# A twelve-layer float32 network on one core: the order of Strassen pairs and second-product units in the FFN blocks

## The chip, the core and the metric

The program runs on one core of one Trainium2 chip. The metric is the device time of one execution in microseconds (us), the median of several runs. TensorE (PE in the views) multiplies; its weight loads are listed apart as PEld. VectorE (DVE), ScalarE (ACT) and GpSimd (POOL) work element by element, and SyncE (SP) issues most of the DMAs. Each engine runs its own instructions in the order in which they were written, and waits at the first one whose inputs are not there.

## The reference

`x` is 512 tokens of 1024 features in float32. A first network of four layers (a gated linear recurrence, a spatial gating unit, a short convolution, a second recurrence) is followed by a second network of one layer (an RWKV-7 scan beside dilated attention, then cross attention to a memory). Every one of the five layers ends in the same feed-forward block (FFN):

```
def _sqrelu_mlp(h, w1, w2):
    return jnp.square(jax.nn.relu(h @ w1)) @ w2      # w1: 1024 x 4096, w2: 4096 x 1024

x = x + mix
x = x + _sqrelu_mlp(_rmsnorm(x, norm_mlp_g[i]), mlp_w1[i], mlp_w2[i])
```

The second network's block is the same with its own names (`ffn_w1_2`, `ffn_w2_2`), and the result is normed once more at the end. The change touches these five FFN blocks alone.

## The kernel before

Activations lie feature by token: a tile of 128 features x 512 tokens fills one of 75 equal slots in SBUF (tag "A", NSLOT = 75), or one of 8 PSUM banks. A float32 product is made of three reduced-precision ones: every operand is split into a rounded part and a rest (hi and lo), and `mm3` issues hi*hi (L896), hi*lo (L897) and lo*hi (L898). Weights come from HBM as float32 `raw` tiles, are rounded on ACT into `whi` (L839 for a whole unit of 128x1024, L825 for half a unit) and the rest goes into `wlo` on DVE (L840, L807).

An FFN block, `ffn`, works in four quarters of 1024 hidden features. `us[q]` holds quarter q as eight tiles, each as `uhi`/`ulo`.

- The first quarter's eight first-product units are plain products (`mm`).
- The other 24 come as 12 Strassen **pairs** (`pair`, letter P in the table): two hidden tiles by seven products of half width (84 matmuls of 128x256; operands `thi`, `tlo`). DVE forms four sums of weight tiles (`ws`, L796 and L798) and seven `wlo`; as products end, DVE adds them up (`cm` L1074 and L1075, `tu` L1078, `cy` L1080 and L1083), ACT does relu (L940), square (L1005) and the rounding into `uhi` (L1006), and DVE makes `ulo` (L1009). A pair's tile j+1 is finished from `tu`, tile j last, from `cy`.
- The second product is made of **units** (`unit`, letter U): 24 matmuls of 128x512 over the eight tiles of `us[q]`, then DVE adds the bank to `x` (L1093). Eight units per quarter. `late` makes a unit of quarters 1 to 3 read the tiles in the order 0..5, 7, 6, since 7 and 6 are finished last.

What stands where is written out by hand: three groups, one per quarter q = 0, 1, 2, each with the eight units of quarter q and the four pairs that make quarter q + 1, in the order of a string of twelve letters (line 1110). After the third group `project` runs the eight units of quarter 3. Within group 0, units also drive `side`, which forms the Strassen operands from the normed input.

Weights are readied ahead: `_next` prepares (rounds) units up to two places ahead of the one in use (PREP = 2, a place is a unit or two products of a pair), and issues loads on SP in the order of use, with at most two whole units and two pairs of raw weights in flight. Stages of several threads (the recurrence layers, the second network's mixing stage and its cross attention) are ordered by a planner (`schedule`), which follows a modelled clock through the whole program; an FFN block has one thread, so its order is only the string's.

Of the kernel before, what the change touches and what calls it, by code (L numbers as in the profile page):

```python
# [651 lines left out]
class Net:  # L652
# [340 lines left out]
    def ffn(self, inp, nxt, w1, w2):  # L993
# [64 lines left out]
        def pair(s0, s1, u, j, last):  # L1058

            a, b = HALF  # L1060
            ps, add = {}, nc.vector.tensor_add
            for i, (k, bank, h) in enumerate(PRODUCTS):
                w = self.w_pair(s0, s1, i)
                while todo and todo[0][0] <= i:
                    todo.pop(0)[1]()
                if h == 0:
                    ps[bank] = self.psum()
                for c in range(4):
                    self.mm3(ps[bank][:, HALF[h]], w[0][:, c], w[1][:, c], *op[k, c], c == 0, c == 3, 357)
                if i == 1:  # L1070
                    y, m = self.t("cy"), self.t("cm")
                    nc.scalar.copy(y[:, a], ps[0][:, a])
                elif i == 2:
                    add(m[:, a], y[:, a], ps[0][:, b])  # L1074
                    add(m[:, b], m[:, a], ps[1][:, a])  # L1075
                elif i == 4:
                    t = self.t("tu")
                    add(t.rearrange("p (c n) -> p c n", c=2), m[:, None, b].to_broadcast([P, 2, 256]),  # L1078
                        ps[2].rearrange("p (c n) -> p c n", c=2))
                    add(y[:, b], m[:, a], ps[2][:, b])  # L1080
                    todo.extend(relu2(t, u, j + 1, (5, 6)))
                elif i == 6:
                    add(y, y, ps[3])  # L1083
                    todo.extend(relu2(y, u, j, (0, 1)))
                    if last:
                        while todo:
                            todo.pop(0)[1]()
                self.lock(i < 6)
                yield

        def unit(q, m):
            ps = yield from self.mm(w2[q][m], us[q], ks=late if q else None)
            nc.vector.tensor_add(self.x[m], self.x[m], ps)  # L1093
            yield
# [12 lines left out]
            yield  # L1107
        for q in range(3):
            u, j, m = us[q + 1], 0, 0
            for step in "UUUUUUPUUPPP" if q == 0 else "UUUUPUUPUUPP":  # L1110
                if step == "P":
                    yield from pair(w1[q * 8 + 8 + j], w1[q * 8 + 9 + j], u, j, j == 6)
                    j += 2
                    continue
                for n, need in enumerate(unit(q, m)):
                    if n % 2 == 1 and todo:
                        todo.pop(0)[1]()
                    if q == 0 and n % 2 == 0:
                        next(side, None)
                    yield need  # L1120
                m += 1
            us[q] = None
# [1056 lines left out]
```

## Time and profile before

| | |
|---|---|
| median of 3 runs | 3479.54 us (3474.63 to 3480.76) |
| profiled execution, its own time | 3475.65 us |
| its span in the trace | 3473.8 us |
| TensorE busy | 3377.3 us, 97% of the span |
| VectorE busy | 2308.4 us, 66% |
| ScalarE busy | 1529.3 us, 44% |
| granted TensorE clock, mean | 0.993 of full speed |

The profiled execution took 3475.65 us, of which the span holds 3473.8; it lies inside the range of the timed runs. PE's busy time hardly tells stages apart: matmuls are pipelined, each is recorded longer than it advances the engine, so what a stretch costs is read from the starts of its first matmul and of the one behind it.

### The profile page before, as it was taken

How to read it: one execution, taken by the hardware profiler on the slowest of the kernel's cores; microseconds unless marked ns; L12 is line 12 of the kernel's file. 1: busy time of each engine (PE TensorE's matmuls, PEld its weight loads, DVE VectorE, ACT ScalarE, POOL GpSimd, SP SyncE). 2: the span in 40 equal slices, each digit the busy share in tenths (PEclk: the TensorE clock that was granted, in tenths of full speed). 3: DMA queues.
4: the chain of work that ended last, by engine and by line, in shares of the span. 5: the costliest groups of instructions: out<-in, count | busy, mean ns of one | idle time of the engine just before them, and what ended most of it. 6: DMA issues, size and time to landing. Idle time of an engine off the chain costs nothing. (4 is left out here: it accounts for less than half of the span.)

```text
span 3473.8 us, 48153 instructions
## 1 busy us (share of the span) xinstructions
PE 3377.3 (97%) x18850; PEld 2778.3 (80%) x18850; DVE 2308.4 (66%) x3618; ACT 1529.3 (44%) x2391; POOL 521.4 (15%) x845
## 2 busy tenths in 40 slices
PE   8999999999999999999999999999999999999998
PEld 6778888888887888888877888777767787778887
DVE  7677666567666567666767666776567666567665
ACT  5634444345443234444554445443354344334444
POOL 1020002210001010002010001556245400110002
PEclk9999999999999999999999999999999999999999
DMA  3223332232333333332224232332224245223331
GB/s 119 87 85 115 97 98 83 84 94 92 98 98 104 97 91 103 98 98 91 82 85 133 73 98 85 109 90 85 73 82 127 87 121 173 64 76 122 94 100 62
DMA packets 127236, 334.90 MB, mean 96 GB/s; under 512 B 18592, under 2 KB 21792, under 8 KB 127008
## 3 DMA queue, kind: packets, MB, share of 16 engines
q1 hardware_dynamic: 119712, 322.37, 30.0%
q0 software_dynamic: 7296, 9.46, 1.1%
q8 instruction: 148, 2.42, 0.3%
q14 instruction: 80, 0.66, 0.1%
HBM read 317.07 MB, written 14.68 MB: 95 GB/s over the span
## 5 line engine op out<-in xcount | busy, mean ns | idle before, releaser
L840 DVE TENSOR_TENSOR wlo<-raw,whi 128x1024 fp32r<-128x1024 f32 (+3 forms) x466 | 608.9, 1307 | 279.3 <-ACT whi L839 270.3
L896 PE MATMUL ps<-hhi,whi 128*128 128x512 f32 x1512 | 619.1, 409 | 11.2 <-ACT whi L839 6.9
L898 PE MATMUL ps<-hhi,wlo 128*128 128x512 f32 x1512 | 598.8, 396 | 7.3 <-DVE wlo L840 7.3
L897 PE MATMUL ps<-hlo,whi 128*128 128x512 f32 x1512 | 599.0, 396 | 5.7 <-DVE hlo L476 5.7
L839 ACT CAST whi<-raw 128x1024 fp32r<-128x1024 f32 (+3 forms) x466 | 463.8, 999 | 309.9 <-PE ps L897 181.7
L896 PE MATMUL ps<-uhi,whi 128*128 128x512 f32 (+1 forms) x1296 | 511.5, 395 | 16.1 <-ACT uhi L1006 16.1
L897 PE MATMUL ps<-ulo,whi 128*128 128x512 f32 (+1 forms) x1296 | 511.3, 395 | 6.1 <-DVE ulo L1009 6.1
L898 PE MATMUL ps<-uhi,wlo 128*128 128x512 f32 (+1 forms) x1296 | 509.6, 393 | 0.0
L898 PE MATMUL ps<-thi,wlo 128*128 128x256 f32 x1680 | 475.1, 283 | 7.8 <-DVE wlo L807 7.1
L897 PE MATMUL ps<-tlo,whi 128*128 128x256 f32 x1680 | 471.8, 281 | 0.0
L896 PE MATMUL ps<-thi,whi 128*128 128x256 f32 x1680 | 471.1, 280 | 0.0
L896 PEld LDWEIGHTS ps<-hhi,whi 128*128 128x128 f32 x1512 | 285.2, 189 | 85.0 <-ACT whi L839 6.9
L898 PEld LDWEIGHTS ps<-hhi,wlo 128*128 128x128 f32 x1512 | 285.1, 189 | 76.2 <-DVE wlo L840 9.0
L897 PEld LDWEIGHTS ps<-hlo,whi 128*128 128x128 f32 x1512 | 285.1, 189 | 71.6 <-DVE hlo L476 10.5
L898 PEld LDWEIGHTS ps<-thi,wlo 128*128 128x128 f32 x1680 | 316.3, 188 | 13.9 <-DVE wlo L807 13.9
L896 PEld LDWEIGHTS ps<-thi,whi 128*128 128x128 f32 x1680 | 316.8, 189 | 1.8
L897 PEld LDWEIGHTS ps<-tlo,whi 128*128 128x128 f32 x1680 | 316.1, 188 | 1.8
L896 PEld LDWEIGHTS ps<-uhi,whi 128*128 128x128 f32 x1296 | 244.9, 189 | 76.5 <-ACT uhi L1006 22.6
L897 PEld LDWEIGHTS ps<-ulo,whi 128*128 128x128 f32 x1296 | 244.9, 189 | 67.1 <-DVE ulo L1009 13.1
L825 ACT CAST whi<-ws 128x512 fp32r<-128x512 f32 x240 | 149.0, 621 | 323.0 <-DVE ws L798 169.6
L898 PEld LDWEIGHTS ps<-uhi,wlo 128*128 128x128 f32 x1296 | 244.8, 189 | 55.7
L897 PE MATMUL ps<-lo,whi 128*128 128x512 f32 x616 | 245.5, 398 | 7.1 <-DVE lo L1258 4.5
(363 smaller groups left out, 4984.2 us busy)
## 6 DMA issues: line engine op xcount, KB each, us to landing
raw<-in_mlp_dram SPq DMA_DIRECT2D x160, 512.0 KB, 3.6
raw<-in_mlp_dram SPq DMA_DIRECT2D x192, 256.0 KB, 5.6
raw<-in_u_ffn_w_dram SPq DMA_DIRECT2D x40, 512.0 KB, 3.6
raw<-in_a_win_dram SPq DMA_DIRECT2D x39, 512.0 KB, 3.6
raw<-in_w_rest_dram SPq DMA_DIRECT2D x34, 512.0 KB, 3.7
raw<-in_w_rkv_dram SPq DMA_DIRECT2D x26, 512.0 KB, 3.6
raw<-in_c_win_dram SPq DMA_DIRECT2D x24, 512.0 KB, 3.6
raw<-in_u_ffn_w_dram SPq DMA_DIRECT2D x48, 256.0 KB, 5.6
```

The source lines that it names most:

```text
L825: nc.scalar.copy(h, w)
L839: nc.scalar.copy(h[:, c], r[:, c])
L840: nc.vector.tensor_sub(l[:, c], r[:, c], rt(h[:, c]))
L896: nc.tensor.matmul(ps, wh, xh, start=start, stop=False)
L897: nc.tensor.matmul(ps, wh, xl, start=False, stop=False)
L898: nc.tensor.matmul(ps, wl, xh, start=False, stop=stop)
```

## The change

The letters are put in another order. In group 0, `UUUUUUPUUPPP` becomes `UUUUUPUPUPPU`; in groups 1 and 2, `UUUUPUUPUUPP` becomes `UUUUPUPUPUPU`. The numbers of units (8) and pairs (4) in a group stay, and each group now ends with a unit.

```
-            for step in "UUUUUUPUUPPP" if q == 0 else "UUUUPUUPUUPP":
+            for step in "UUUUUPUPUPPU" if q == 0 else "UUUUPUPUPUPU":
```

In the built program the places look like this.

ACT in the first FFN block, from the last pair of group 0 to the first unit of group 1, before (`whi<-raw 128x1024` is the rounding of a unit's weights, `tu` and `cy` end in the two hidden tiles):

```order
L1072 COPY cy<-ps 128x256
L825 CAST whi<-ws 128x512
L839 CAST whi<-raw 128x1024
L940 ACTIVATE tu<-tu 128x512
L1005 ACTIVATE tu<-tu 128x512
L1006 CAST uhi<-tu 128x512
L839 CAST whi<-raw 128x1024
L940 ACTIVATE cy<-cy 128x512
L1005 ACTIVATE cy<-cy 128x512
L1006 CAST uhi<-cy 128x512
```

The same place now:

```order
L1072 COPY cy<-ps 128x256
L839 CAST whi<-raw 128x1024 x2
L940 ACTIVATE tu<-tu 128x512
L1005 ACTIVATE tu<-tu 128x512
L1006 CAST uhi<-tu 128x512
L940 ACTIVATE cy<-cy 128x512
L1005 ACTIVATE cy<-cy 128x512
L1006 CAST uhi<-cy 128x512
L839 CAST whi<-raw 128x1024 x3
```

The unit of group 0 that now stands behind the pair, and the first one of group 1, have both been rounded before the pair's last tiles come, and no rounding of a unit stands between the two tiles any more.

DVE in group 1 of the same block, from the `tu` of the first pair on, before, where two units follow (`x<-x,ps` closes a unit):

```order
L1078 TENSOR_TENSOR tu<-cm,ps 128x512
L1080 TENSOR_TENSOR cy<-cm,ps 128x256
L840 TENSOR_TENSOR wlo<-raw,whi 128x1024
L1009 TENSOR_TENSOR ulo<-tu,uhi 128x512
L1083 TENSOR_TENSOR cy<-cy,ps 128x512
L796 TENSOR_TENSOR ws<-raw 128x512
L798 TENSOR_TENSOR ws<-ws,raw 128x512
L807 TENSOR_TENSOR wlo<-raw,whi 128x512
L798 TENSOR_TENSOR ws<-raw 128x512
L1009 TENSOR_TENSOR ulo<-cy,uhi 128x512
L1093 TENSOR_TENSOR x<-x,ps 128x512
```

The same place now, where one unit follows and then the next pair:

```order
L1078 TENSOR_TENSOR tu<-cm,ps 128x512
L1080 TENSOR_TENSOR cy<-cm,ps 128x256
L796 TENSOR_TENSOR ws<-raw 128x512
L798 TENSOR_TENSOR ws<-ws,raw 128x512
L807 TENSOR_TENSOR wlo<-raw,whi 128x512
L798 TENSOR_TENSOR ws<-raw 128x512
L1009 TENSOR_TENSOR ulo<-tu,uhi 128x512
L1083 TENSOR_TENSOR cy<-cy,ps 128x512
L807 TENSOR_TENSOR wlo<-ws,whi 128x512 x2
L1009 TENSOR_TENSOR ulo<-cy,uhi 128x512
L1093 TENSOR_TENSOR x<-x,ps 128x512
```

The next pair's first weight sums have moved ahead of this pair's last additions.

The planner's clock reaches the second network's mixing stage at another moment, and there it chooses another order; one place on ACT (`p` is a projected tile, + is now, - is before):

```order
-L1481 ACTIVATE p<-z,vec 128x512
 L1481 ACTIVATE p<-z,vec 32x512
 L839 CAST whi<-raw 128x1024
+L1481 ACTIVATE p<-z,vec 128x512
+L939 ACT_TABLE_LOAD
+L940 ACTIVATE p<-p 128x512
+L940 ACTIVATE p<-p 32x512
+L945 CAST hi<-p 128x512
+L945 CAST hi<-p 32x512
 L1634 COPY bkT<-ps 128x512
```

An activation has moved ahead of the copies, and brings a load of ACT's function table with it; there are two more such loads in the whole program. The recurrence layers keep their order.

## Rows read from the trace of the kernel before

**Rows 1.** The page's part 1: engine, busy us, share, instructions.
```profile
PE 3377.3 (97%) x18850; PEld 2778.3 (80%) x18850; DVE 2308.4 (66%) x3618; ACT 1529.3 (44%) x2391; POOL 521.4 (15%) x845
```
**Rows 2.** Who waited for whom, PE alone, whole run: total, times, longest.
```profile
PE ps L896 <- ACT uhi L1006: 16.1, 15, 1.8
...
PE ps L898 <- DVE wlo L807: 7.1, 25, 0.5
PE ps L897 <- DVE ulo L1009: 6.1, 19, 0.6
```
**Rows 3.** Stretches: length, busy PE, PEld, DVE, ACT, POOL, clock, DMA, GB/s; 2190.07: mixing.
```profile
282.98:591.51 308.53, 302.41 (x1778) 264.49 (x1776) 208.99 (x314) 139.75 (x223) 18.52 (x14) 0.99 0.31 99
783.31:1090.28 306.97, 301.01 (x1778) 263.66 (x1776) 209.27 (x315) 139.81 (x223) 17.27 (x21) 1.00 0.31 97
1314.04:1622.07 308.03, 301.92 (x1778) 264.54 (x1777) 209.36 (x315) 139.84 (x223) 17.25 (x20) 0.99 0.30 96
1881.45:2190.07 308.62, 302.89 (x1778) 264.66 (x1777) 204.85 (x315) 144.26 (x231) 27.15 (x18) 0.99 0.32 98
2190.07:3150.27 960.20, 934.26 (x5939) 709.49 (x5938) 629.51 (x1228) 398.20 (x674) 304.69 (x652) 1.00 0.33 99
3150.27:3412.76 262.49, 257.30 (x1585) 228.45 (x1584) 179.47 (x288) 123.47 (x202) 0.00 (x0) 0.99 0.30 95
```
**Rows 4.** Stretches of the first FFN block, from letter to letter.
```profile
282.98:316.32 33.34, 33.34 (x146) 27.05 (x144) 25.07 (x43) 14.39 (x24) 0.00 (x0) 1.00 0.54 174
316.32:326.23 9.91, 9.91 (x86) 9.91 (x85) 6.69 (x11) 4.24 (x7) 0.00 (x0) 1.00 0.24 81
...
337.31:369.37 32.06, 30.81 (x253) 29.99 (x252) 26.67 (x46) 18.63 (x33) 0.00 (x0) 1.00 0.01 1
369.37:396.75 27.38, 24.72 (x98) 19.04 (x97) 11.81 (x17) 9.09 (x13) 0.00 (x0) 0.94 0.48 154
...
438.98:459.28 20.30, 20.11 (x169) 19.90 (x168) 16.26 (x28) 11.79 (x20) 0.00 (x0) 1.00 0.01 1
459.28:483.01 23.73, 22.82 (x99) 17.95 (x98) 11.87 (x17) 8.15 (x12) 0.00 (x0) 1.00 0.55 178
...
545.49:591.51 46.02, 45.11 (x195) 35.95 (x193) 30.53 (x28) 16.37 (x21) 18.52 (x14) 1.00 0.41 125
```
**Rows 5.** PE in time order in group 1's first unit: start, us, idle before.
```profile
374.56 0.50 PE L897 MATMUL ps<-ulo,whi 128*128 128x512 f32 x1 [0.59 <-DVE ulo L1009]
...
377.13 0.49 PE L896 MATMUL ps<-uhi,whi 128*128 128x512 f32 x1 [1.84 <-ACT uhi L1006]
```
**Rows 6.** Shorter stretches of the same units, with the clock.
```profile
369.37:377.00 7.63, 5.33 (x23) 3.68 (x21) 3.09 (x5) 4.64 (x8) 0.00 (x0) 1.00 0.46 146
377.00:382.00 5.00, 4.64 (x12) 3.49 (x13) 3.65 (x4) 2.07 (x3) 0.00 (x0) 0.66 0.88 283
```
**Rows 7.** ACT and DVE in time order, tile 6 behind group 0's pairs.
```profile
376.46 0.62 ACT L1006 CAST uhi<-cy 128x512 fp32r<-128x512 f32 x1
377.11 0.69 DVE L1009 TENSOR_TENSOR ulo<-cy,uhi 128x512 fp32r<-128x512 f32 x1 [2.01 <-ACT uhi L1006]
```
**Rows 8.** DVE in time order, inside the three pairs, and in the units behind.
```profile
357.52 0.68 DVE L807 TENSOR_TENSOR wlo<-raw,whi 128x512 fp32r<-128x512 f32 x1
358.12 0.68 DVE L798 TENSOR_TENSOR ws<-raw 128x512 f32<-128x512 f32 x1
...
378.06 1.23 DVE L840 TENSOR_TENSOR wlo<-raw,whi 128x1024 fp32r<-128x1024 f32 x1 [0.26 <-ACT whi L839]
379.20 0.68 DVE L1093 TENSOR_TENSOR x<-x,ps 128x512 f32<-128x512 f32 x1
```
**Rows 9.** Who waited for whom, SP's queue, a pair's raw weights: total, times, longest.
```profile
SPq L760 <- DVE ws L798: 62.5, 5, 12.8
```
**Rows 10.** The line that loads ACT's table: ns, first and last start.
```profile
L939 ACT ACT_TABLE_LOAD  x33: 1283/1283/1283, 26.3 to 2980.5; - x33
```

## The prediction, before the kernel was run

> **What bounds the kernel now.** I read the page's busy shares first: PE is busy for 97% of the span, DVE, the next, for 66% [rows 1]. So TensorE bounds nearly everywhere, and a new order of the same matmuls can only win where PE stands still or runs slowly. The next view is the list of what PE waited for. Two of its larger entries belong to the FFN blocks: the rounding of finished hidden tiles (uhi, 15 waits, 16.1 us) and their rests (ulo, 19 waits, 6.1 us); wlo of L807, the weights of pairs, adds 25 short waits, 7.1 us [rows 2]. Fifteen is five blocks times three groups: it is the end of each group.
>
> Idle time alone understates it, so the third view is the table of stretches. A stretch here runs from the first matmul of a letter's kind to the first of the next kind. Six units take 33.34 us without a wait, which is 5.56 us each; a pair alone takes 9.91 us [rows 4]. A block has 32 units and 12 pairs: 32 x 5.56 + 12 x 9.91 = 296.8 us if nothing waits. The four whole blocks took 308.53, 306.97, 308.03 and 308.62 us; the fifth, up to its last eight units, took 262.49 us [rows 3], against 262.51 in the first block (545.49 - 282.98), so it is like the first. The surplus is 11.7, 10.2, 11.2, 11.8 and 11.7 us, 56.6 us in all. That is the most that the order of letters can give back.
>
> Where it lies, in the first block [rows 4]:
> - group 0 to 1: four units in 27.38 us instead of 22.24, surplus 5.1;
> - group 1 to 2: 23.73 instead of 22.24, surplus 1.5;
> - group 2 to the last eight: 46.02 instead of 44.48, surplus 1.5;
> - the three pairs in a row: 32.06 instead of 29.73, surplus 2.3;
> - two pairs in a row, at two places alike: 20.30 instead of 19.82, surplus 1.0 together.
>
> That is 11.4 of the 11.7.
>
> **The end of a group.** Group 0 ends with PPP. Its last product ends at 369.37; tile 7 of the next quarter (from tu) and tile 6 (from cy) are then still on their way through DVE and ACT. The first unit reads them as its seventh and eighth operand, that is 6 x 0.695 = 4.2 and 4.9 us later (a unit's 5.56 us over eight operands). The trace shows PE waiting 0.59 for ulo of tile 7, then 1.84 for uhi of tile 6 [rows 5]. Tile 6's uhi ends at 376.46 + 0.62 = 377.08, 7.7 us behind the last product, its ulo at 377.80, 8.4 behind [rows 7]. PE is idle for 27.38 - 24.72 = 2.66 of the 5.1 us [rows 4]; most of the rest is clock: in the 5 us that follow, the granted clock is 0.66 on average, a mix of the two levels 2.4 and 1.2 GHz, after 1.0 before [rows 6]. At the other two ends, the short wait costs 1.5 us with the clock at 1.00 in the table.
>
> The new order puts one unit of the old quarter between the last pair and the first unit of the new one. It needs only tiles that are long finished. So tiles 7 and 6 are needed 5.56 us later: uhi of tile 6 at 4.9 + 5.6 = 10.4 us behind the last product, its ulo at 10.7. Had they the lateness of the worst case above, 7.7 and 8.4 us, they would still be early by 2.3 us or more; at the other ends, where PE is idle for 0.91 in all (23.73 - 22.82) [rows 4], by more than 4. The rounding of the extra unit stands ahead of the tiles on ACT, as the rows on the change show, and adds nothing between them. I take the three surpluses as gone: 8.1 us per block in four of the blocks; in the second it was 6.5, since its surplus is 1.5 smaller.
>
> **Pairs in a row.** A pair asks DVE for 15 operations of 512 columns and three of 256. DVE starts one of 512 every 0.60 us when it has no wait (357.52, 358.12) [rows 8]; with an estimate of 0.38 for a short one, between half that pitch and the whole, a pair is 15 x 0.60 + 3 x 0.38 = 10.1 us of DVE, more than its 9.91 us of PE, so pairs in a row fall behind; a pair and a unit are 10.1 + 1.14 (wlo L840, 378.06 to 379.20) + 0.6 (x) = 11.8 us of DVE [rows 8] against 15.47 of PE. With PUPU this backlog is worked off after every pair. The two PP of groups 1 and 2 are gone, and PPP of group 0 becomes PP behind a P U. That one keeps a surplus between the 0.5 of a PP after two units and the 2.3 of PPP; it has less rest ahead than a PP had, so I take 1.0.
>
> **What the change adds.** In a block, eight pairs now stand right behind a single unit (two in group 0, three in each other group); none did before. Their first two products are readied only from the last product of the pair ahead: 1.4 + 5.6 = 7 us before use instead of 11. In that time DVE has nine operations of 512 columns (the last rows on the change), 5.4 us. It fits, by 1.6 us. If it doesn't, the matmul of L898 waits for wlo, and behind it the whole PE queue: the nearest row is the wait for L807, 0.28 us on average and 0.5 at the longest [rows 2]. Bounds 0 to 0.5 each; the queue fits, so I take 0.05, 0.4 per block. The first pair of group 0 comes one unit earlier: DVE was busy 25.07 of 33.34 us there [rows 4], and now has some 23.3 (less one unit's 1.74) in 27.8; bounds 0 to 0.5 us, I take 0.2. Loads: the SP queue issues the same number in the order of use; raw weights of pairs are wanted later than they are issued by 20 us and more, and units in a row keep their rhythm, so nothing.
>
> So a block keeps 1.0 + 0.4 + 0.2 = 1.6, and with 0.1 for the rest 1.7 us of its surplus: 5 x 1.7 = 8.5. Gain in the blocks: 56.6 - 8.5 = 48 us.
>
> **The mixing stage.** The planner reorders it as a side effect. PE is idle there 960.20 - 934.26 = 26 us [rows 3]. Two more table loads of 1.283 us [rows 10] on an ACT that is 41% busy may or may not show. Without an argument for a sign, the bounds are a gain of 10 and a loss of 20 us (less than half of its idle time gone, or four fifths of it added); I take a loss of 3, by the table loads.
>
> **Sum.** 48 - 3 = 45 us. The profiled execution's own 3475.65 becomes 3430.6; the median of the runs shown is 3.9 us above it, so 3434.5 us.
>
> **A rule against the change.** The stall repeats at the same place of every group, and PE's waits there were ended by ACT and DVE, not by a load or a buffer [rows 2, 5]; a load of a pair's weights waited for a slot only five times, once per block [rows 9]. The Trainium skill, Perfetto Trace Analysis, Identifying the Most-Contended Engine, says that the same gap coming back on the engine that should be full can mean that there isn't room for the next tile. By that rule the change would not help, since it holds two quarters' hidden tiles at once up to the end of a group; that is the last rival below. The trace does not agree with it here.
>
> **Rivals.**
> 1. The chain at a group's end gets longer, and the unit covers half. For it: ACT and DVE work for the extra unit, too; against: 2.3 us of margin. Gain 24 - 3 = 21: 3458 us.
> 2. The new plan of the mixing stage costs its upper bound, 20 us: 3479.5 - 48 + 20 = 3452 us. For it: it was reordered throughout; against: the same planner with the same rules.
> 3. Slower: DVE's margin of 1.6 us at a single unit isn't there. The in-order queue holds the next pair's wlo behind the sums and additions that wait for PE, at 40 pairs (8 x 5). It decides from 45 / 40 = 1.1 us per pair on. At the price of the worst stall seen, 1.84 [rows 5], it is 74 us: 3434 + 74 = 3508 us. Against it: 11.8 of 15.47 us of DVE.
> 4. Slots: loads of pairs wait for tiles still held, and PE stands as long as before: 3480 us. Counted along the built order, at most 70 of the 75 slots are held at once (69 before), so it is unlikely.
>
> **Chances.** My forecast 0.80, rival 1 0.08, rival 2 0.06, rival 3 0.04, rival 4 0.02. A measurement here tells 0.2% (7 us) from no change. Faster is the forecast with rivals 1 and 2, 0.94; same is rival 4, 0.02; slower is rival 3, 0.04. The range of the forecast goes from the whole surplus gone with 6 us gained in the mixing stage (3417) to rival 2 (3452); a little of rival 1 is taken in, to 3454.
>
> **What would show it.** PE's waits for uhi L1006 vanish from the list, and the four units at a group's head take 22.3 us at a clock of 1.00. The pairs PP of group 0 take 20.3 to 21.5 us. A pair behind a single unit starts without a wait, and a block takes 298 to 299 us. I am wrong if L807 or L825 takes the place of uhi in PE's list, or if the mixing stage moves by more than 15 us from 960.

## The result, and the profile after

The changed kernel takes 3442.68 us (median of 4 runs, 3440.15 to 3443.86); the kernel before, beside it, took 3480.15 us (4 runs, 3474.63 to 3486.31). The ratio is 0.9891 with an interval of 0.9873 to 0.9908: 37.5 us less. The profiled execution took 3442.72 us, its span 3441.0 us. The forecast was 3434.5 us, range 3417 to 3454. So the direction holds, and the time is 8 us above the forecast: 37.5 us were gained where 45 were expected.

The page's part 1 answers to [rows 1]: PE is busy for a point more of a shorter span, and no other engine has come near it.

```profile
PE 3368.1 (98%) x18850; PEld 2780.3 (81%) x18850; DVE 2308.0 (67%) x3618; ACT 1536.0 (45%) x2393; POOL 526.1 (15%) x845
```

PE's waits over the whole run (engine, line, releaser: total, times, longest), which answer to [rows 2]:

```profile
PE ps L896 <- ACT hi L945: 4.6, 1, 4.6
...
PE ps L883 <- DVE rhs L1734: 2.1, 4, 0.7
...
PE ps L898 <- DVE wlo L807: 1.3, 5, 0.3
```

The waits for uhi and ulo are gone from the list, and of the 25 waits for a pair's wlo five are left, one per block. New is a single wait of 4.6 us for a rounding at L945. It lies in the second network's mixing stage, behind the last normalisation of the scan; near the same place the kernel before waited twice, 1.54 and 2.48 us.

The stretches that answer to [rows 3] (length, busy PE, PEld, DVE, ACT, POOL, clock, DMA share, GB/s): the four whole blocks, and the mixing stage.

```profile
284.58:582.50 297.92, 297.68 (x1777) 263.74 (x1776) 208.66 (x314) 140.97 (x223) 18.61 (x14) 1.00 0.32 103
774.08:1072.04 297.96, 297.69 (x1778) 263.35 (x1776) 208.88 (x315) 140.98 (x223) 17.27 (x21) 1.00 0.30 100
1295.61:1593.74 298.13, 297.89 (x1778) 263.61 (x1776) 208.94 (x315) 140.73 (x223) 17.22 (x20) 1.00 0.31 99
1854.48:2152.78 298.30, 298.05 (x1778) 263.43 (x1776) 203.60 (x314) 144.96 (x230) 27.10 (x18) 1.00 0.31 101
2152.78:3128.57 975.79, 944.38 (x5939) 712.96 (x5938) 631.17 (x1228) 399.97 (x676) 309.53 (x652) 0.99 0.32 97
```

The four blocks gave back 10.6, 9.0, 9.9 and 10.3 us. The fifth, with its last eight units, went from 305.1 to 294.1 us (from the first matmul on a hidden tile to the one behind the last unit), 11.0 us. That is 50.9 us. The mixing stage got longer by 975.79 - 960.20 = 15.6 us. The stages between, whose order did not change, and the start add some 2.4; 50.9 - 15.6 - 2.4 = 32.9, as the profiled executions differ (3475.65 - 3442.72). (Of those 2.4 nothing is explained here: the first stage alone, from the first matmul to the first on a hidden tile, took between 274.4 and 278.5 us in all these profiles, always in the same order.)

Pieces of the first block, as in [rows 4]: UUUUU, the PP of group 0, the last U of group 0 with four of group 1, and the last nine units.

```profile
284.58:312.37 27.79, 27.79 (x121) 22.55 (x120) 23.00 (x41) 13.34 (x23) 0.00 (x0) 1.00 0.56 189
...
343.37:363.80 20.43, 20.19 (x170) 19.98 (x168) 16.85 (x29) 12.00 (x21) 0.00 (x0) 1.00 0.00 1
363.80:391.55 27.75, 27.75 (x123) 22.53 (x121) 13.79 (x19) 9.12 (x13) 0.00 (x0) 1.00 0.61 208
...
532.35:582.50 50.15, 50.15 (x218) 40.55 (x217) 31.45 (x28) 17.09 (x22) 18.61 (x14) 1.00 0.40 122
```

Length equals busy PE in every row but that of PP: PE stands still for 0.24 us in the whole block. A group's head now runs at 27.75 / 5 = 5.55 us per unit. Tile 6 behind group 0, which answers to [rows 7] (start, us, engine, line):

```profile
368.87 0.62 ACT L1006 CAST uhi<-cy 128x512 fp32r<-128x512 f32 x1
...
369.53 0.69 DVE L1009 TENSOR_TENSOR ulo<-cy,uhi 128x512 fp32r<-128x512 f32 x1 [2.02 <-ACT uhi L1006]
```

Its uhi is there 369.49 - 363.80 = 5.7 us behind the pair's last product and its ulo 6.4; they are first wanted 5.55 + 4.9 = 10.4 us behind. The 5 us at the place of [rows 6] have no dip of the clock left:

```profile
371.42:376.42 5.00, 5.00 (x23) 4.08 (x22) 2.71 (x4) 0.23 (x1) 0.00 (x0) 1.00 0.60 179
```

SP's queue now waits more often for the slot of a pair's raw weights, and PE does not notice. Before, there were the five waits of [rows 9] and five more in a row of their own:

```profile
SPq L760 <- DVE wlo L807: 8.9, 5, 1.8
```

Now:

```profile
SPq L760 <- DVE wlo L807: 82.4, 10, 15.0
SPq L760 <- DVE ws L798: 41.3, 16, 3.1
```

### The profile page after: what moved, and what is told of

Its sections match the earlier page's. It is cut to its first block, busy times and chain, and to the rows that moved or that the text cites. A ratio compares the mean times of both kernels' runs of the same rounds, so it can differ in the third digit from the quotient of the medians.

```text
span 3441.0 us, 48118 instructions
## 1 busy us (share of the span) xinstructions
PE 3368.1 (98%) x18850; PEld 2780.3 (81%) x18850; DVE 2308.0 (67%) x3618; ACT 1536.0 (45%) x2393; POOL 526.1 (15%) x845
## 5 line engine op out<-in xcount | busy, mean ns | idle before, releaser
L840 DVE TENSOR_TENSOR wlo<-raw,whi 128x1024 fp32r<-128x1024 f32 (+2 forms) x466 | 609.4, 1308 | 278.6 <-ACT whi L839 269.4
L839 ACT CAST whi<-raw 128x1024 fp32r<-128x1024 f32 (+2 forms) x466 | 463.3, 999 | 383.0 <-PE ps L897 215.7
L896 PE MATMUL ps<-hhi,whi 128*128 128x512 f32 (+1 forms) x1512 | 621.2, 411 | 11.3 <-ACT whi L839 6.1
L898 PE MATMUL ps<-hhi,wlo 128*128 128x512 f32 (+1 forms) x1512 | 600.0, 397 | 6.9 <-DVE wlo L840 6.9
L897 PE MATMUL ps<-hlo,whi 128*128 128x512 f32 (+1 forms) x1512 | 601.6, 398 | 5.3 <-DVE hlo L476 5.2
L896 PEld LDWEIGHTS ps<-hhi,whi 128*128 128x128 f32 (+1 forms) x1512 | 286.3, 189 | 85.7 <-ACT hhi L475 6.6
L898 PEld LDWEIGHTS ps<-hhi,wlo 128*128 128x128 f32 (+1 forms) x1512 | 286.4, 189 | 75.3 <-DVE wlo L840 8.4
L897 PEld LDWEIGHTS ps<-hlo,whi 128*128 128x128 f32 (+1 forms) x1512 | 286.5, 189 | 71.0 <-DVE hlo L476 10.4
L896 PE MATMUL ps<-hi,whi 128*128 128x512 f32 x616 | 248.5, 403 | 7.5 <-ACT hi L945 4.6
```

The costliest lines, as they stand in the source:

```text
L839: nc.scalar.copy(h[:, c], r[:, c])
L840: nc.vector.tensor_sub(l[:, c], r[:, c], rt(h[:, c]))
L896: nc.tensor.matmul(ps, wh, xh, start=start, stop=False)
L897: nc.tensor.matmul(ps, wh, xl, start=False, stop=False)
L898: nc.tensor.matmul(ps, wl, xh, start=False, stop=stop)
```

## The experiments

Theory: the blocks gained what was forecast, and the planner's new order of the mixing stage costs what is missing. Rival: the stage is slower in one execution by chance, or the blocks gain less than their stretches say. Each kernel was compared with the kernel before on its own chip. In the profiles of the edited kernels the line numbers of the code shown are 5 higher, in those of the last two edits 8 higher.

**The two halves of the change, one at a time: block order and planned order.** The strings of the blocks (GROUPS) and the strings for which the planner plans the stages of several threads (PLAN_GROUPS) were made two settings:

```
+GROUPS = ('UUUUUPUPUPPU', 'UUUUPUPUPUPU')
+PLAN_GROUPS = ('UUUUUUPUUPPP', 'UUUUPUUPUUPP')
-            for step in "UUUUUPUPUPPU" if q == 0 else "UUUUPUPUPUPU":
+            for step in GROUPS[q > 0]:
...
+    order = [a if m else b for m, a, b in zip(many, plans[0][0], plans[1][0])]
```

New order in the blocks, planned stages ordered as before:

> The FFN blocks in the changed order, but the planned stages (recurrence layers, mixing stage, cross attention) in the order that the planner chose for the kernel before. Theory: the planner's new order of the mixing stage costs the 15.6 us by which that stage grew (960.2 to 975.8), and the blocks gain 51 us; then the mixing stage is back at 960 +- 2 and the time is 3480 - 51 = 3429 us. Rival: the stage grew for another reason (what the changed blocks leave behind in queues or clock); then it stays near 976 and the time near 3443 us.

Measured: 3432.33 us (3429.81 to 3444.01), ratio 0.9869 [0.9855, 0.9883]. The median is near the theory's 3429, but the one profile is of the longest of these runs, 3444.01 us, and its mixing stage took the rival's time:

```profile
2154.00:3129.10 975.10, 948.67 (x5939) 718.29 (x5938) 631.60 (x1228) 398.77 (x674) 305.07 (x652) 0.98 0.32 97
```

The granted clock was 0.98 over this stage, against 1.00 in the kernel before; where it dipped is told at the end. So this profile does not decide, and the stage had to be looked at again. The opposite, old strings in the blocks and the new plan:

> The reverse: FFN blocks in the order of before, planned stages in the changed kernel's order. Theory (the order of the mixing stage costs 15.6 us by itself): 3480 + 15.6 = 3496 us, mixing stage 976. Rival (something that the changed blocks leave behind): 3480 us, mixing stage 960.

Measured: 3489.51 us (3487.78 to 3492.07), ratio 1.0025 [1.0016, 1.0035]: slower than before by 9.0 us, with its mixing stage at

```profile
2188.96:3163.32 974.36, 943.51 (x5939) 711.98 (x5938) 628.79 (x1228) 400.00 (x676) 309.00 (x652) 0.99 0.32 98
```

Both medians lie between the theory's number and the rival's: the plan costs, but by these times some 9 to 10 us, not the 15.6 of one profile. So the changed kernel and the first edit were run again, on one chip:

> The changed kernel itself, on the same chip as the next three. Both theories: 3442 to 3443 us as timed before; its mixing stage 974 to 977 us with the wait of TensorE for ACT's rounding (hi, L945) of 4.6 us near the stage's end in the profile.

> The new order in the FFN blocks with the mixing stage in the order of before, a second time. Theory (the plan's side effect costs 9 to 10 us): 3431 to 3434 us, 9 to 11 us below the changed kernel on the same chip, and a mixing stage of 960 to 965 us in a profile without a long dip of the clock. Rival (the first measurement was luck, the plans are worth the same): 3440 to 3443 us.

Measured: 3440.03 us (3439.47 to 3444.21) and 3430.87 us (3428.01 to 3437.15), 9.2 us apart; against before 0.9884 [0.9869, 0.9899] and 0.9858 [0.9841, 0.9874]. Their mixing stages, first of the changed kernel:

```profile
2153.15:3129.11 975.96, 944.58 (x5939) 712.75 (x5938) 629.18 (x1228) 400.09 (x676) 308.99 (x652) 0.99 0.32 97
```

and then of the one with the stage ordered as before:

```profile
2153.58:3113.21 959.63, 935.47 (x5939) 710.38 (x5938) 629.16 (x1228) 398.59 (x674) 308.21 (x652) 1.00 0.32 99
```

So the stage's length follows its order (976 against 960 us), in several executions and with either order in the blocks; the one exception is the profile above, with the clock at 0.98. The rival is out. Both were measured a third time, each beside the kernel before:

> The changed kernel once more on the chip of the edited one, to compare with: 3439 to 3443 us, with the 4.6 us wait. Both theories say the same.

> The new order in the FFN blocks with the mixing stage in the order of before, a third time, on the chip of the run ahead: 3430 to 3434 us by both theories; it gives the distance of the edited kernel from the best one.

Measured: 3443.08 us (before 3480.51; ratio 0.9895 [0.988, 0.991]; stage 975.2) and 3427.46 us, below what was expected (before 3480.20; ratio 0.9853 [0.9834, 0.9872]; stage 959.3). Against before on their own chips, the changed kernel gains 37.5, 38.5 and 37.4 us; without the new plan it gains 48.1, 47.7 and 52.7. This is the best version here: 3427 to 3432 us.

**The end unit alone.** Group 0 `UUUUUUPUPPPU`, groups 1 and 2 `UUUUPUUPUPPU`, planned stages as before:

> Only a unit moved to each group's end, the pairs otherwise as before: UUUUUUPUPPPU, UUUUPUUPUPPU, planned stages in the order of before. Theory: one unit of 5.56 us covers the end of a group even behind three pairs in a row, so the three waits for uhi and ulo vanish with the clock loss behind the first (39 us in all five blocks), and PPP keeps its 2.3 us and PP its 0.5: 3480 - 39 = 3441 us. Rival: behind three pairs in a row the last tiles are later than the unit covers; then group 0 keeps half of its 5.1 us, 3480 - 39 + 12 = 3453 us.

Measured: 3444.17 us (3443.43 to 3446.90), ratio 0.9898 [0.9885, 0.9911], a gain of 36.3. PPP, the head of group 1 with the unit ahead of it, and the first block:

```profile
331.34:363.55 32.21, 30.84 (x254) 30.02 (x253) 27.29 (x47) 18.88 (x34) 0.00 (x0) 1.00 0.01 1
363.55:391.19 27.64, 27.64 (x123) 22.53 (x121) 13.72 (x19) 10.05 (x14) 0.00 (x0) 1.00 0.53 171
...
282.53:583.13 300.60, 298.51 (x1777) 263.68 (x1776) 209.22 (x315) 140.03 (x223) 18.62 (x15) 1.00 0.31 102
```

The ends are clean, five units in 27.64 us; PPP keeps its surplus (32.21 - 29.73 = 2.5). No wait for uhi or ulo is left in PE's list. That also decides the forecast's first rival: even behind PPP one unit covers the chain.

**The alternation alone.** All groups `UUUUUPUPUPUP`, so that each ends with a pair, planned stages as before:

> Only the alternation, each group still ending with a pair: UUUUUPUPUPUP in all three groups, planned stages in the order of before. Theory: the last tiles still come 5 to 6 us behind the last product and are wanted after 4.2 and 4.9, so each end keeps a short wait of 0.9 us and 1.5 us of surplus; the long one of group 0 shrinks to that, since no pairs stand in a row; pairs lose nothing. Gain 56.6 - 15 x 1.5 - 2 = 32: 3448 us. Rival: the waits came from the backlog of pairs in a row alone; then the ends are clean too, gain 52 to 55, 3427 us.

Measured: 3454.97 us (3452.28 to 3465.74), ratio 0.9933 [0.992, 0.9945], a gain of 25.5 where 32 was expected. The head of group 1 (that of group 2 took 29.76 us), and the first block:

```profile
366.03:395.83 29.80, 28.43 (x122) 22.45 (x121) 13.06 (x17) 8.96 (x13) 0.00 (x0) 1.00 0.54 187
...
281.79:584.93 303.14, 299.04 (x1777) 263.39 (x1776) 209.84 (x315) 141.46 (x224) 18.56 (x14) 1.00 0.31 101
```

The head of five units takes 29.8 instead of 27.75 us, 2.0 more where 1.5 was taken; at 15 heads that is 8 us, about what the gain falls short by. PE's waits, of the same kernel, show the chain at the end in its pure form, without a backlog of pairs:

```profile
PE ps L901 <- ACT uhi L1011: 16.7, 15, 1.1
```

It waits 15 times, 1.1 us each; the pairs' wlo is not among the waits. Gains of 36.3 and 25.5 are 61.8 together, more than the 48 to 53 of both at once: they overlap at the end of group 0, whose surplus of 5.1 us falls to 2.0 by the alternation alone and to nothing by the unit alone.

**Other plans.** New order in the blocks, planned stages in the orders that the planner finds for two other pairs of strings:

> The new order in the FFN blocks; the planned stages in the order that the planner finds for the strings of the end-unit kernel. In that order the eight products of the memory values (v) are added up ahead of the last normalisation of the scan by as many operations as in the changed kernel (14 on VectorE between the last v and the last y; 5 in the kernel before). Theory (the loss comes from this filler work being used up early): the 4.6 us wait is there, 3441 to 3444 us. Rival (the loss lies in the rest of the new order, where this one has 1483 differing rows on TensorE against the changed kernel): anything else, 3431 to 3436 us.

> The new order in the FFN blocks; the planned stages in the order found for the strings of the alternating kernel. It is the order of before up to the last normalisation of the scan (415 differing rows on TensorE), but all eight products of the memory values stand behind that normalisation. Theory (filler beside the last normalisation covers it): no wait of over 3 us for ACT's rounding there, and 3430 to 3434 us, as with the order of before. Rival (the order of before is good by chance of its tuning and any other costs as much): 3440 us or more.

Measured: 3441.04 us (3439.87 to 3442.28), ratio 0.9884 [0.987, 0.9899], stage 974.8; and 3443.55 us (3438.32 to 3450.24), ratio 0.9895 [0.9879, 0.9911]. The first is what the theory said, with a wait of 4.6 us. The second has the rival's time. Its profile is of the longest of its runs, 3450.24 us, with a stage of 983.3. In it the last normalisation is covered, but 27 us ahead of it, in the scan, PE ran out of other work. Its waits:

```profile
PE ps L888 <- DVE S L1757: 4.6, 3, 3.7
...
PE ps L888 <- DVE rhs L1739: 3.8, 5, 1.7
```

and the stretch in which the longest of them lie, with the one behind it:

```profile
2790.00:2800.00 10.00, 4.27 (x34) 3.22 (x32) 7.58 (x16) 1.70 (x3) 0.00 (x0) 0.70 0.37 104
2800.00:2820.00 20.00, 20.00 (x126) 15.89 (x126) 6.68 (x19) 3.49 (x6) 0.00 (x0) 0.55 0.18 54
```

After 5.7 us of idle time PE runs for 20 us at a mean clock of 0.55. The longest wait is for the scan's state S, and DVE's queue shows why: six rests of normalised tiles (3.69 us), a short operation and the rest of a unit's weights (1.21 us) stand ahead of S, which DVE starts at 2794.15 us.

**Moving cover back to the last normalisation.** The order of the changed kernel's mixing stage was edited near its end, and nothing else. First the memory's steps (kv; chain is the scan, norm its last normalisation, m1 the attention merge, m2 the rest; xN is N steps):

```
-chain kvx7 chain kvx7 chain kvx7 chain kvx7 chain m1 kv chain kv chainx5 norm m1x3 normx3 m1x3 m2x4 normx2 m2x2 norm m2x4 normx4 m2...
+chain kvx3 chain kvx3 chain kvx3 chain kvx3 chain m1 chainx6 norm m1x3 kvx4 normx3 m1x3 kvx6 m2x4 normx2 kvx2 m2x2 norm kvx4 m2x4 norm kvx2 normx3 m2...
```

> The changed kernel with one edit in the order of the mixing stage: the last 18 steps of the memory's keys and values (kv) are moved from between the scan's last steps to beside the last normalisation (54 rows of TensorE moved, nothing else). Theory (the last normalisation lost its cover): the 4.6 us wait for ACT's rounding shrinks to below 2.6, the clock there stays at 1.00, the stage takes 968 to 971 us instead of 976, and the time falls by 4 to 7 us below the changed kernel, to 3434 to 3437 us; the other 3 to 5 us of the plan's cost remain, since they lie elsewhere. Rival (filler work is short altogether, so its wait comes back between the scan's last steps, which lost it): a wait for S, rhs or Z of 2 us or more appears some 30 to 60 us earlier, and the time stays within 2 us of the changed kernel, 3439 to 3443 us.

Measured: 3444.01 us (3441.99 to 3446.11), ratio 0.9898 [0.9882, 0.9915], stage 976.3: no gain. That is the rival's time, and no gain beside the changed kernel on the same chip (3443.08), but not by the rival's mechanism. PE's waits:

```profile
PE ps L904 <- ACT hi L953: 5.3, 1, 5.3
...
PE ps L891 <- DVE rhs L1742: 2.7, 5, 0.7
...
PE ps L891 <- DVE Z L1749: 1.8, 5, 0.7
```

No long wait came back in the scan (rhs and Z together grew by 1.0 us); the one at the end grew from 4.6 to 5.3 us. ACT's rows of the normalisation's first and last step show that the chain began earlier and ended no sooner; in the changed kernel

```profile
2853.17 0.59 ACT L1773 ACTIVATE ysq<-ps 128x512 f32<-128x512 f32 x1
...
2865.08 0.62 ACT L945 CAST hi<-y 128x512 fp32r<-128x512 f32 x1 [3.78 <-DVE y L1788]
```

and in the edited one

```profile
2850.20 0.59 ACT L1781 ACTIVATE ysq<-ps 128x512 f32<-128x512 f32 x1
...
2865.92 0.62 ACT L953 CAST hi<-y 128x512 fp32r<-128x512 f32 x1 [2.82 <-DVE y L1796]
```

The chain got longer, from 11.9 to 15.7 us. First on ACT and then on DVE, this stands in it:

```profile
2855.85 0.63 ACT L948 ACTIVATE ld<-ld 128x512 f32<-128x512 f32 x1 [3.46 <-DMA ld<-gd]
...
2858.26 1.22 DVE L848 TENSOR_TENSOR wlo<-raw,whi 128x1024 fp32r<-128x1024 f32 x1 [3.43 <-ACT whi L847]
```

ACT stands for 3.46 us at an activation of m2 whose tile is still being loaded. The rounding of a unit's weights comes behind that on ACT, the rest of these weights waits for it on DVE, and the chain's next step there stands behind: it starts at 2859.41 us, 5.7 behind PE's last product for it, where it was 0.8 in the changed kernel (2858.57). The cover's own copies and additions are in these queues, too, but the chain does not wait for them: behind each, ACT or DVE stands idle again for 1.7 us or more. Nor does the length of the chain decide by itself. With the order of before (second run of the first edit) the same steps take 22.9 us, 2828.11 to 2850.97, and PE waits for 1.56 and 2.47 us, since other products fill the time.

Then the attention merge, which stands there in the kernel before:

```
-... chain m1 kv chain kv chainx5 norm m1x3 normx3 m1x3 m2x4 normx2 m2x2 norm m2x4 normx4 m2...
+... chain kv chain kv chainx5 norm m1 normx3 m1x2 normx2 m1x2 norm m1 norm m1 normx3 m1x3 m2...
```

(Three more m1 steps are moved away from between kv steps ahead of it.)

> The changed kernel with one other edit at the end of the mixing stage: not the memory's products but the last ten steps of the attention merge (L1917 to L1920, some 1.4 us of TensorE for each of its products) are moved beside and behind the last normalisation, where they stand in the kernel before (26 rows of TensorE moved). Theory (that merge is the missing cover): the 4.6 us wait for ACT's rounding shrinks to 2.5 or less, no wait of 2 us or more takes its place among the scan's last steps, and the time falls by 3 to 6 us, to 3435 to 3439 us; the rest of the plan's cost stays. Rival (the 4.6 us wait is no more than a part of what the order of before waits there too, and the plan's cost is spread over the stage): 3439 to 3443 us, whatever becomes of that wait.

Measured: 3459.85 us (3456.57 to 3465.39), ratio 0.9941 [0.9928, 0.9955]: 17 us slower than the changed kernel, with a stage of 989.4 us; neither the theory nor the rival had that. PE's waits:

```profile
PE ps L891 <- DVE rhs L1742: 6.6, 6, 2.4
...
PE ps L891 <- DVE S L1760: 5.4, 3, 2.6
...
PE ps L891 <- DVE Z L1749: 3.4, 4, 2.2
...
PE ps L905 <- DVE lo L954: 1.8, 1, 1.8
```

The 4.6 us wait fell to 0.65 and 1.8 us, but five waits of 2.1 to 2.6 us appeared between the scan's last steps. The same 40 us of the stage's end, in the changed kernel

```profile
2833.00:2873.00 40.00, 34.91 (x219) 28.88 (x219) 21.91 (x38) 18.19 (x26) 0.00 (x0) 0.91 0.45 152
```

and here

```profile
2833.00:2873.00 40.00, 30.80 (x185) 26.30 (x184) 12.49 (x25) 13.64 (x20) 0.00 (x0) 0.82 0.29 99
```

My theory's first clause held, and the other two failed. DVE was busy for only 12.49 of these 40 us, and yet it is its queue that makes PE wait; one of the five places on DVE:

```profile
2835.84 1.23 DVE L848 TENSOR_TENSOR wlo<-raw,whi 128x1024 fp32r<-128x1024 f32 x1 [5.59 <-ACT whi L847]
2836.99 0.22 DVE L1742 TENSOR_TENSOR rhs<-ps,av 128x64 f32<-128x64 f32 x1
```

The scan's step stands behind the rest of a unit's weights. That waits 5.59 us for ACT's rounding of these weights, which itself waited for PE's products ahead; the other four places look the same (1.79 to 5.46 us). The order leaves PE no other product until the scan's step is there. So in the three kernels in which a long wait came up or grew (the plan of the alternating kernel and these two edits), a step of the chain was held in DVE's in-order queue, each time behind the rest of a unit's weights, among other work. That the stage's work as cover is a fixed stock, which the chains share, would be another reading; it was not tested apart. No single wait is "the" cost of the new plan.

## Why the prediction was right, and which term was off

- **The end of a group.** Right, and safer than forecast. Tile 6 is ready 5.7 and 6.4 us behind the last product, not 7.7 and 8.4; the margin is 4.7 us at uhi and 4.3 at ulo, where the forecast's numbers give 2.7 and 2.3. The 2 us come from the place of the roundings on ACT. With the end unit alone, a unit's rounding still stands between the two tiles, and DVE waits for it ahead of tile 6's last addition; in the changed kernel that rounding comes before both tiles, and DVE's same row waits for nothing:

```profile
366.83 1.23 DVE L845 TENSOR_TENSOR wlo<-raw,whi 128x1024 fp32r<-128x1024 f32 x1 [2.63 <-ACT whi L844]
...
364.44 1.22 DVE L840 TENSOR_TENSOR wlo<-raw,whi 128x1024 fp32r<-128x1024 f32 x1
```

  The prediction read this order, and gave it no price. With the end unit alone tile 6 is still 7.7 and 8.4 us late, and that unit covers it. The end unit alone is worth 36.3 us in the medians, where the forecast's three ends make 38.9 (four times 8.1 and 6.5).
- **Pairs in a row.** PP of group 0 takes 20.43 us, a surplus of 0.6 where 1.0 was taken, in the announced 20.3 to 21.5.
- **Pairs behind a single unit.** DVE's time is enough: in the first block these pairs take 9.95 to 9.96 us against 9.91, and none begins with a wait. Rival 3, slower by DVE's queue, is out; of L807 five waits of 0.2 to 0.3 us are left, in the first block inside PP. How much of the margin of 1.6 us is left was not measured.
- **The block.** 297.9 to 298.3 us, at the lower edge of the announced 298 to 299. The five blocks keep 56.6 - 50.9 = 5.7 us where 8.5 was taken, by the two points above. In the medians the blocks alone, with the stage ordered as before, give 47.7 to 52.7 us; 48 was forecast.
- **Slots, and the rule against the change.** The Trainium skill, Perfetto Trace Analysis, Optimization Strategy (the prediction names the section ahead of it), says that such a repeating gap can mean missing room. The trace does not bear that out here: loads of pairs wait for slots more often than before (26 waits in the two rows above, against 10 in the same two before), yet the gap is gone; its waits had been for ACT and DVE. The prediction counted only the five waits of [rows 9] and left out the five behind L807.
- **The mixing stage: the term that was mis-sized.** A loss of 3 us was taken, for two table loads. It is 15.6 us between the two profiles, 9.2 us between the medians on one chip, and by the gains against before some 12 on average (49.5 - 37.8). That lies inside the bounds (a gain of 10 to a loss of 20), but the profile crossed the 15 us that the forecast had named as a sign of being wrong. Giving the two loads the whole price was the mistake. In the last normalisation, where the new order has a load (2856.72 to 2858.00 us in the changed kernel), ACT is through with it and still idle for 1.34 us until DVE delivers. Between profiles of the two orders (975.96 and 959.63 us, on one chip), idle PE is 975.96 - 944.58 = 31.4 against 959.63 - 935.47 = 24.2 us, 7.2 more; the remaining 9.1 lie in busy time. Two places show. The first is where PE waits for POOL's `G` (L1686), 1.64 us, and the clock falls behind that wait; first the new order (second run of the changed kernel), then that of before (second run of the first edit):

```profile
2360.00:2400.00 40.00, 38.21 (x269) 27.64 (x270) 25.33 (x72) 11.17 (x25) 17.12 (x44) 0.91 0.27 83
...
2360.00:2400.00 40.00, 39.42 (x363) 28.75 (x363) 26.64 (x72) 11.99 (x25) 21.63 (x52) 1.00 0.31 91
```

  The second is the last normalisation. Behind the 4.6 us wait the clock falls, to 0.91 over the 40 us shown above and to 0.96 over the same 40 us in the second run; the order of before, with 4.23 us idle in all, keeps 1.00:

```profile
2833.00:2873.00 40.00, 34.84 (x229) 28.84 (x228) 23.81 (x42) 16.77 (x25) 0.00 (x0) 0.96 0.50 165
...
2815.00:2855.00 40.00, 35.77 (x233) 29.44 (x231) 27.40 (x44) 22.40 (x34) 0.00 (x0) 1.00 0.49 171
```

  By an estimate from these rows the clock costs 40 x 0.09 + 40 x 0.04 = 5.2 us, and idle time 1.2 + 0.9 = 2.1, so the two places hold some 7 of the 16.3 us. The dip at the first place is not in every execution: the profile of the changed kernel above has the wait, 1.58 us, and a clock of 1.00 behind it. Where the other 9 us arise was not found, and the edits at the stage's end gave none of the loss back.

So, by the averages of the medians, 49.5 us came from the blocks where 48 was forecast, and the plan took about 12 of them instead of 3: 38 us instead of 45. The mechanism in the blocks was the one forecast; the stage's price had no argument in the forecast, and its size was off by about a factor of four.

## What to carry to other kernels

Where an in-order engine meets freshly finished operands at a boundary, one unit of old work put behind the last producer is worth its place; read from the trace how far behind the last product the slowest operand comes, and compare it with when it is first read. Where a planner with an absolute clock orders a later stage, a small edit ahead of it reshuffles that stage: hold its plan fixed and time both changes apart, since here the second took back about a quarter of the first. And before moving independent work to cover one chain, ask which chain it covers now, and what stands ahead of the chain's own steps in the in-order queues of the helper engines.

## What the runs showed of the hardware that was not expected

- The clock dipped without idle time ahead of it. In the profiled run of the new order with the old plan, these stretches of the mixing stage follow each other:

```profile
2541.00:2567.00 26.00, 25.97 (x196) 18.53 (x196) 18.64 (x32) 19.78 (x34) 7.20 (x13) 1.00 0.30 92
2567.00:2588.00 21.00, 21.00 (x95) 12.65 (x94) 9.82 (x21) 10.54 (x17) 13.99 (x39) 0.51 0.45 148
```

  PE was busy for 25.97 of 26 us, and then ran for 21 us at a mean clock of 0.51, near the lower of its two levels: some 21 x 0.49 = 10 us lost. The same part of the stage in the second run of the same kernel had 1.00:

```profile
2553.00:2593.00 40.00, 39.64 (x291) 25.89 (x289) 29.38 (x56) 23.74 (x41) 26.56 (x61) 1.00 0.54 180
```

  The profile with the plan of the alternating kernel, whose order is nearly the same up to there, has the dip at the same place:

```profile
2565.00:2586.00 21.00, 21.00 (x93) 12.61 (x94) 9.76 (x21) 10.66 (x17) 14.95 (x42) 0.51 0.43 146
```

  What sets it off was not found. Single runs of the new order with the old plan lie up to 15 us apart (3425.43 to 3440.99 in the third measurement, at mean clocks of 0.994 and 0.989). That the medians on one chip differ by 9 us where the profiles of the stage differ by 16 is in part the choice of the profiled runs: one was 3443.22 us, with a median of 3440.03, the other 3429.33, with a median of 3430.87. The rest may be such dips in some of the runs; that was not shown.
- Here a wait cost more than its length. In the alternating kernel PE was idle for 29.80 - 28.43 = 1.37 us at a group's head and the head took 2.0 us longer, with the granted clock at 1.00 in the table; in the kernel before, 0.91 us of idle time cost 1.5 [rows 4].
